# A hybrid decoder layer on one core: where the recurrent mixers stand beside the input projection, and how many tiles share a reciprocal root

## The chip, the cores and the metric

The kernel runs on one core of a Trainium2 chip. The metric is the device time of one execution in microseconds (us). The engines are TensorE (PE, with its weight loads shown as PEld), VectorE (DVE), ScalarE (ACT) and GpSimd (POOL); SyncE (SP) issues most DMAs. Each engine works through its own instructions in a fixed order and waits where an operand, a buffer or a DMA is not there yet. PE's granted clock is given as a share of full speed.

## The reference

One layer over 2048 tokens of width 1024, all in float32:

```python
h = _rms(x, norm_mix_g)
z = h @ w_in + b_in                       # 3600 columns
(a_q, a_k, a_v, a_f, b_qk, b_v, b_i, b_f, b_o, c_q, c_f, c_i, c_g) = _split_cols(z)
oa = _fox_attention(_rms(a_q), _rms(a_k), a_v, cumsum(log_sigmoid(a_f)))    # 8 heads of 64
qb, kb = split(silu(causal_conv4(b_qk)))
ob = _mlstm_chunkwise(qb, kb, b_v, b_i, b_f)                                # 4 heads of 64
oc = _hgrn2_chunkwise(silu(c_q), logf(c_f), c_i)                            # 4 heads of 64
y  = concat(_rms(oa)*g, sigmoid(b_o)*_rms(ob)*g, silu(c_g)*_rms(oc)*g)
x  = x + y @ w_out
x  = x + conv_glu(_rms(x, norm_ffn_g), w_up, ffn_conv_w, ffn_conv_b, w_down)
```

mLSTM (`ob`) and HGRN2 (`oc`) are recurrent: a block of tokens needs the state that the block before left. Both need only their own columns of z. A head of the attention needs the q, k and v of all 2048 tokens.

## The kernel before

**Projection.** z is made in two halves of 1024 tokens. A half is two token blocks of 512, whose x tiles (128 tokens each) are loaded, normed, transposed on PE and split into a high and a low part (`z_norm`, `norm_to_T`). `z_groups` then goes through 14 column groups in the order of the table `ORDER[hf]`. The weights of a group come in through the two buffers `wraw`, are cast on ACT and split on POOL (`load_split`); every product is three matmuls (`mm3`, high x high, high x low, low x high). Ten groups (`nat_group`) put tokens on the partitions and take 192 matmuls of up to 264 columns; b0, b1, c0 and c1 (`ct_group`) put columns there and take 96 matmuls of 512. A half is thus 2304 matmuls, all of them on one line, L166. bo, ci, cg, bv, b0, b1, c0 and c1 feed the recurrent mixers, k0, k1, q0, q1, v0 and v1 the attention; either set is 1152 matmuls a half. Results go to DRAM (`s_n`, `s_bqk`, `s_c`, `s_qh`, `s_kh`, `s_v` and so on) and are read back from there. A q or k tile is first normed per head of 64 (`qk_norm_T`): a reciprocal root on DVE in a chain of dependent small instructions (`rms_scale`, L109 to L120), one chain for each tile of 256 tokens.

**Mixers.** `mixers` runs four blocks of 512 tokens, each `phase_b` (mLSTM) with `phase_c` (HGRN2); a block starts when its eight groups are ready. Their tiles in PSUM are called b.

**Attention.** `attention` goes head by head in two passes, row maxima first and scores behind them; the first pass leads by 22 steps (`LEAD`). It begins when both halves are projected, since the pools of the projection are closed first. Then come w_out and the gated feed-forward part.

**What sets the order.** `merge(main, side, rate)` writes out `rate` steps of the mixers for each step of the projection; what is left of the mixers is written out with the attention, two of its steps for each of theirs. A scheduler in the build then fixes each engine's order by a simulated timeline of its own, among what the buffers allow. Before, half 0 is projected by itself, with the mixers' groups first; half 1 is projected with the mixers beside it, the attention's groups first:

```python
for _ in z:
    pass
merge(z_groups(k, 1, pz, wp, psw, (xb, xw)), mix, RZ)      # RZ = 2.5
...
for _ in mix:
    for _ in range(RA):                                    # RA = 2
        next(att, None)
```

The x tiles of half 0 and of half 1's first block go through buffers of the mixers' pool (v and p4, four in all), those of half 1's second block through wraw.

Of the kernel before, what the change touches and what calls it, by code (L numbers as in the profile page):

```python
# [9 lines left out]
F32 = mybir.dt.float32  # L10
F32R = mybir.dt.float32r
# [3 lines left out]
AF = mybir.ActivationFunctionType  # L15
ALU = mybir.AluOpType
# [23 lines left out]

RZ, RA = 2.5, 2

# [5 lines left out]
    "bo ci cg bv b0 b1 c0 c1 k0 k1 q0 q1 v0 v1",  # L48
    "k0 k1 q0 q1 v0 v1 ci cg bo bv b0 b1 c0 c1",
)  # L50
# [71 lines left out]

def norm_to_T(k, pool, psum, ptag, x, gb, hi, lo, tok, xn=None):

    nc = k.nc
    ss = k.t(pool, [P, 1], tag="nss")
    if xn is None:
        xn = k.t(pool, [P, D], tag="xn")
        junk, src = xn, x
    else:  # L130
        junk, src = lo[:, :, tok : tok + P], x.rearrange("p (a t) -> p a t", t=P)
    nc.scalar.activation(junk, src, AF.Square, accum_out=ss)
# [36 lines left out]
def z_norm(k, hf, b, pz, psum, xbufs):  # L169

    hi = k.t(pz, [P, DT, BLK], F32R, tag="hhi")
    lo = k.t(pz, [P, DT, BLK], F32R, tag="hlo")
    for tt in range(4):
        t0 = hf * HALF + b * BLK + tt * P
        xp, tag, bufs = xbufs[tt % len(xbufs)]
        x = k.t(xp, [P, D], tag=tag, bufs=bufs)
        k.nc.sync.dma_start(x, k.a["x"][0, t0 : t0 + P, :])
        if t0 == 0:
            k.nc.sync.dma_start(k.gmix, k.a["norm_mix_g"][0:1, :].broadcast_to([P, D]))
        norm_to_T(k, pz, psum, "t", x, k.gmix, hi, lo, tt * P, xn=x)  # L180
    return hi, lo


def z_groups(k, hf, pz, wp, psum, xbufs):
# [22 lines left out]
    def nat_group(off, kind, g):  # L207
# [6 lines left out]
        for b in range(2):  # L214
# [3 lines left out]
            for tp in range(2):  # L218
# [80 lines left out]

def qk_norm_T(k, pz, psum, z, kind, g, t0):  # L300
# [4 lines left out]
    z8 = z.rearrange("p tt (h d) -> p (tt h) d", d=HD)  # L305
    nc.scalar.activation(sq, z8, AF.Square)
    ss = k.t(pz, [P, 8], tag="ss")
    nc.vector.tensor_reduce(ss, sq, axis=AX.X, op=ALU.add)
    rstd = k.t(pz, [P, 8], tag="rstd")
    rms_scale(k, pz, rstd, ss, HD, 1.0, "h")  # L310
    nc.gpsimd.tensor_tensor(z8, z8, rstd.unsqueeze(2).broadcast_to([P, 8, HD]), op=ALU.mult)
    gcol = k.gq if kind == "q" else k.gk
    dhi, dlo = (k.s_qh, k.s_ql) if kind == "q" else (k.s_kh, k.s_kl)
    ps = k.t(psum, [P, 2, 2 * P], tag="t", bufs=2)
    for c in range(2):
        for tt in range(2):
            nc.tensor.transpose(
                ps[:, c, tt * P : (tt + 1) * P],
                z[:, tt, c * P : (c + 1) * P],
                k.ident,  # L320
            )
    lo = k.t(pz, [P, 2, 2 * P], F32R, tag="l", bufs=2)
    nc.scalar.activation(hi, ps, AF.Copy, scale=gcol)
    nc.vector.scalar_tensor_tensor(lo, ps, gcol, hi.bitcast(F32), op0=ALU.mult, op1=ALU.subtract)
    for dst, src in ((dhi, hi), (dlo, lo)):
        nc.sync.dma_start(
            dst[g * 256 : (g + 1) * 256, t0 : t0 + 2 * P].rearrange("(c p) t -> p c t", p=P), src.bitcast(F32)
        )

# [1002 lines left out]
def _trunk(ctx, tc, a, out):  # L1332
# [37 lines left out]
    with ExitStack() as ms:  # L1370
# [13 lines left out]
        with ExitStack() as zs:  # L1384
# [6 lines left out]
            next(z)  # L1391
            pz.tile([P, 8], F32, tag="padz", name="padz", bufs=1)
            state(k, mconst)
# [93 lines left out]
def consts(k, a, cp, mconst, pz, psum, cm):  # L1487
# [102 lines left out]
```

## Time and profile before

| | |
|---|---|
| median of 3 runs | 2981.64 us (2981.16 to 2985.46) |
| the profiled execution's own time | 2982.74 us |
| its span | 2981.0 us |
| PE busy, over the span | 2834.5 us (95%) |
| DVE, ACT, POOL busy | 2055.0 (69%), 1255.0 (42%), 1412.5 us (47%) |
| mean granted clock of PE | 0.975 |

The shares are averages over stages with different limits, so the stages have to be read one by one. Here the layer is cut at the times where one kind of work ends: half 0's mixers' groups to 220 us, half 0's attention's groups to 372, half 1's attention's groups to 585, half 1's mixers' groups to 820, attention with mixers beside it to 1143, attention alone to 1490, and the rest to the end.

### The profile page before, as it was taken

The page shows a single profiled execution, that of the slowest core. Times are in us where ns is not written, and L with a number is a line of the kernel's source. Part 1 is how long each engine was busy: PE and PEld are TensorE (multiplying, and loading weights), DVE is VectorE, ACT ScalarE, POOL GpSimd, SP SyncE. Part 2 cuts the span into 40 slices and gives each one's busy share as a digit, 9 for nine tenths or more (in the row PEclk, how much of TensorE's full clock was granted, in tenths as well). Part 3 has the DMA queues.
Part 4 walks back from the last instruction along what each step waited for, and adds up shares of the span by engine and source line. Part 5 has one row for each costly group of instructions (what it writes and reads, how often), then busy time and mean ns, then how long its engine had stood idle before and what let it go on. Part 6 is the DMA issues. An engine that isn't in the chain of part 4 may idle for free. (4 is left out here: it accounts for less than half of the span.)

```text
span 2981.0 us, 43125 instructions
## 1 busy us (share of the span) xinstructions
PE 2834.5 (95%) x15181; PEld 2350.0 (79%) x15181; DVE 2055.0 (69%) x3637; ACT 1255.0 (42%) x2138; POOL 1412.5 (47%) x1149
## 2 busy tenths in 40 slices
PE   7999999899978988899999999999999999999999
PEld 7889989899766665566688778888878888888887
DVE  6426688757379886777746567777697677777655
ACT  3232332312225456677623344444454344444443
POOL 2233434643245556756501176666476544444443
PEclk9999999999988889999999999999999999999999
DMA  5333434433261334433056634544677433333666
GB/s 170 115 113 123 148 106 128 144 93 94 93 149 49 77 66 97 100 71 66 18 182 212 198 129 163 161 157 155 222 263 260 155 105 105 100 102 124 226 206 214
DMA packets 332025, 406.88 MB, mean 136 GB/s; under 512 B 31010, under 2 KB 219504, under 8 KB 328640
## 3 DMA queue, kind: packets, MB, share of 16 engines
q1 hardware_dynamic: 296192, 335.37, 37.5%
q10 hardware_dynamic: 33264, 60.37, 5.4%
q0 software_dynamic: 2352, 8.39, 1.0%
q8 instruction: 119, 1.95, 0.3%
q14 instruction: 98, 0.80, 0.1%
HBM read 276.05 MB, written 127.98 MB: 136 GB/s over the span
## 5 line engine op out<-in xcount | busy, mean ns | idle before, releaser
L1027 POOL TENSOR_TENSOR w<-w,w 128x512 fp32r<-128x512 f32 x302 | 405.0, 1354 | 400.2 <-ACT w L1026 286.1
L1215 PE MATMUL ps<-w,w 128*128 128x512 f32 x1848 | 421.2, 390 | 4.4 <-ACT w L1206 1.9
L1215 PEld LDWEIGHTS ps<-w,w 128*128 128x128 f32 x1848 | 346.6, 188 | 78.2 <-POOL w L1208 2.6
L166 PE MATMUL w<-whi,hhi 128*128 128x256 f32 (+1 forms) x1280 | 369.4, 289 | 2.1 <-DVE pg L228 1.5
L166 PE MATMUL w<-wlo,hhi 128*128 128x256 f32 (+1 forms) x1280 | 367.7, 288 | 0.6 <-POOL wlo L157 0.6
L166 PE MATMUL w<-whi,hlo 128*128 128x256 f32 (+1 forms) x1280 | 367.0, 287 | 0.0
L783 POOL TENSOR_TENSOR pl<-pf,ph 128x512 fp32r<-128x512 f32 (+1 forms) x224 | 269.3, 1214 | 175.6 <-ACT ph L780 113.0
L1208 POOL TENSOR_TENSOR w<-w,w 128x512 fp32r<-128x512 f32 x154 | 215.4, 1405 | 204.4 <-ACT w L1206 172.3
L1026 ACT ACTIVATE w<-w 128x512 fp32r<-128x512 f32 x302 | 180.7, 627 | 261.0 <-POOL w L1027 82.5
L1207 DVE TENSOR_TENSOR w<-w,w 128x512 fp32r<-128x512 f32 x154 | 180.5, 1182 | 104.7 <-ACT w L1205 103.2
L166 PEld LDWEIGHTS w<-whi,hhi 128*128 128x128 f32 x1280 | 246.9, 193 | 3.7 <-issue 2.0
L166 PEld LDWEIGHTS w<-wlo,hhi 128*128 128x128 f32 x1280 | 246.7, 193 | 1.8 <-POOL wlo L157 1.0
L166 PEld LDWEIGHTS w<-whi,hlo 128*128 128x128 f32 x1280 | 246.4, 193 | 0.2
L745 DVE TENSOR_REDUCE mx<-m 128x1 f32<-128x512 f32 (+2 forms) x320 | 188.3, 604 | 63.6 <-PE m L740 36.2
L778 ACT ACTIVATE pf<-s 128x512 f32<-128x512 f32 (+1 forms) x320 | 168.4, 539 | 144.1 <-DVE pl L783 49.9
L157 POOL TENSOR_TENSOR wlo<-wraw,whi 128x1024 fp32r<-128x1024 f32 (+1 forms) x56 | 137.9, 2483 | 170.6 <-ACT whi L156 167.7
L1032 DVE TENSOR_TENSOR w<-w,w 128x512 f32<-128x512 f32 x176 | 151.2, 878 | 81.5 <-DMA w<-in_w_up_dram 69.4
L780 ACT ACTIVATE ph<-pf 128x512 fp32r<-128x512 f32 (+1 forms) x320 | 178.1, 575 | 45.8 <-PE pv L798 38.5
L1073 DVE SCALAR_TENSOR_TENSOR u<-ps,fcol,u 128x1023 f32<-128x1023 f32 x88 | 108.9, 1278 | 91.6 <-ACT u L1072 91.6
L771 PE MATMUL s<-QB,KB 70*128 70x512 f32 (+1 forms) x320 | 134.1, 419 | 30.7 <-ACT pf L778 30.3
L740 PE MATMUL m<-KB,QB 70*128 70x512 f32 (+2 forms) x320 | 135.3, 438 | 21.1 <-DVE mx L745 12.4
L1206 ACT ACTIVATE w<-w 128x512 fp32r<-128x512 f32 x154 | 96.7, 628 | 114.3 <-PE ps L1215 89.5
(349 smaller groups left out, 7102.1 us busy)
## 6 DMA issues: line engine op xcount, KB each, us to landing
w<-in_w_up_dram SPq DMA_DIRECT2D x182, 256.0 KB
w<-s_g SPq DMA_DIRECT2D x154, 256.0 KB
w<-in_w_down_dram SPq DMA_DIRECT2D x110, 256.0 KB
wraw<-in_w_in_dram SPq DMA_DIRECT2D x48, 512.0 KB
s_g<-u ACTq DMA_DIRECT2D x88, 256.0 KB
w<-s_w SPq DMA_DIRECT2D x88, 256.0 KB
s_g<-w ACTq DMA_DIRECT2D x66, 256.0 KB
w<-s_h SPq DMA_DIRECT2D x48, 256.0 KB
```

Source lines behind the costliest of these rows:

```text
L157: nc.gpsimd.tensor_tensor(lo[:, q : q + n, :], raw, h.bitcast(F32), op=ALU.subtract)
L166: nc.tensor.matmul(out, lsl(lhs[a], i), rsl(rhs[b], i), start=(i == 0 and j == 0), stop=(i == n - 1 and j == 2))
L745: nc.vector.tensor_reduce(mx[:, i, kb : kb + 1], ps[:, 0:n], axis=AX.X, op=ALU.max)
L778: nc.scalar.activation(pf[:, c0:], ps[:, c0:], AF.Exp)
L780: nc.scalar.activation(ph[:, c0:], pf[:, c0:], AF.Copy)
L783: eng.tensor_tensor(pl[:, c0:], pf[:, c0:], ph[:, c0:].bitcast(F32), op=ALU.subtract)
L1026: nc.scalar.activation(h, t, AF.Copy)
L1027: nc.gpsimd.tensor_tensor(lo, t, h.bitcast(F32), op=ALU.subtract)
L1032: nc.vector.tensor_tensor(t, x, y, op=op)
L1207: nc.vector.tensor_tensor(gl, gr, gh.bitcast(F32), op=ALU.subtract)
L1208: nc.gpsimd.tensor_tensor(wl, wr, wh.bitcast(F32), op=ALU.subtract)
L1215: nc.tensor.matmul(tiles[tile], g[x][:, tile * P : (tile + 1) * P], w[y], start=j == 0 and c == 0, stop=j == nj - 1 and c == 2,)
```

## The change

1. Half 1 projects the mixers' groups first, like half 0, and its attention's groups in another order.
2. The mixers are merged into the projection from half 0 on, at 2.2 steps for each step of the projection, and at 4.7 steps once c1 of half 1's first block has been projected (`k.ready["c1"] >= 3`).
3. Reciprocal roots are made for several tiles in one chain: two q or k tiles (16 columns in place of 8), and the x tiles that there are buffers for (4 in half 0's second block, 2 in half 1). All tiles of a chain are held until it is done.
4. Both blocks of half 1 take their x tiles through the two wraw buffers.

```diff
-RZ, RA = 2.5, 2
+RZ0, RZ1, RA = 2.2, (2.2, 4.7), 2
 ORDER = (
     "bo ci cg bv b0 b1 c0 c1 k0 k1 q0 q1 v0 v1",
-    "k0 k1 q0 q1 v0 v1 ci cg bo bv b0 b1 c0 c1",
+    "bo ci cg bv b0 b1 c0 c1 v1 v0 k0 q0 k1 q1",
 )
+def norms_to_T(k, pool, psum, ptag, xs, gb, hi, lo, tok):
+    nc = k.nc
+    n = len(xs)
+    ss = k.t(pool, [P, 4], tag="nss")[:, 0:n]
+    for i, x in enumerate(xs):
+        t = tok + i * P
+        nc.scalar.activation(
+            lo[:, :, t : t + P], x.rearrange("p (a t) -> p a t", t=P), AF.Square, accum_out=ss[:, i : i + 1]
+        )
+    rstd = k.t(pool, [P, 4], tag="nrs")[:, 0:n]
+    rms_scale(k, pool, rstd, ss, D, 1.0, f"n{n}")
+    for i, x in enumerate(xs):
+        nc.vector.scalar_tensor_tensor(x, x, rstd[:, i : i + 1], gb, op0=ALU.mult, op1=ALU.mult)
+        to_T(k, psum, ptag, x, hi, lo, tok + i * P)
...
+    n = 1 if hf == b == 0 else sum(bufs for _, _, bufs in xbufs)
+    for t in range(0, 4, n):
...
-                    qk_norm_T(k, pz, psum, z, kind, g, t0)
+                    if tp == 0:
+                        zs, ss = [], k.t(pz, [P, 16], tag="ss")
+                    zs.append((z, qk_squares(k, pz, z, ss[:, 8 * tp : 8 * tp + 8]), t0))
+                    if tp == 1:
+                        qk_norm_T(k, pz, psum, zs, ss, kind, g)
...
-        due += rate
+        due += rate()
...
-            for _ in z:
-                pass
-            merge(z_groups(k, 1, pz, wp, psw, (xb, xw)), mix, RZ)
+            merge(z, mix, lambda: RZ0)
+            merge(z_groups(k, 1, pz, wp, psw, (xw, xw)), mix, lambda: RZ1[k.ready["c1"] >= 3])
```

What the edits make of the order shows at three places. The first is PE in half 0's k1, at the 1248th matmul of the projection, where before only matmuls of the projection (w) stand:

```order
L166 MATMUL w_2066<-wlo_1972,hhi_106 128x256
L166 MATMUL w_2066<-whi_1971,hlo_107 128x256
L166 MATMUL w_2148<-whi_1971,hhi_482 128x256
L166 MATMUL w_2148<-wlo_1972,hhi_482 128x256
L166 MATMUL w_2148<-whi_1971,hlo_483 128x256
```

At the same place the changed kernel has mixers' matmuls (b) between two tiles of the projection (whose line is now L185):

```order
L185 MATMUL w_2111<-wlo_2013,hhi_106 128x256
L185 MATMUL w_2111<-whi_2012,hlo_107 128x256
L530 MATMUL b_2203<-b_qk_1876 128x128
L530 MATMUL b_2204<-b_qk_1876 128x128
L678 MATMUL b_2213<-q_94,c_2093 128x128 x4
L185 MATMUL w_2224<-whi_2012,hhi_482 128x256
L185 MATMUL w_2224<-wlo_2013,hhi_482 128x256
```

Of the mixers' 728 matmuls before (182 for a block), half 0's attention's groups had none beside them, half 1's first 1152 projection matmuls had 198, its last 1152 had 184, and 346 came behind the projection. Now the four numbers are 192, 186, 253 and 97.

The second place is PE at the boundary of the halves, behind half 0's last projection matmul (w_3861). Before, the transposes of the first x tile (t, out of v) stand there, then mixers' matmuls, and the first matmul of half 1 (w_4089) comes before the second x tile's transposes (out of p; some of the mixers' rows between are left out):

```order
L166 MATMUL w_3861<-whi_3469,hlo_483 128x264
L265 MATMUL w_3900<-ident,pg_3764 36x128 x3
L140 MATMUL t_3941<-ident,v_3923 128x128 x4
L140 MATMUL t_3948<-ident,v_3923 128x128 x4
L452 MATMUL b_4205<-ident,rows_4200 128x12 x4
L615 MATMUL b_4428<-q_94,c_4415 128x256 x2
L166 MATMUL w_4089<-whi_4076,hhi_3921 128x256
L166 MATMUL w_4089<-wlo_4077,hhi_3921 128x256
L140 MATMUL t_3973<-ident,p_462_3955 128x128 x4
```

Now two x tiles (out of wraw) stand ahead of that matmul here, and the other two ahead of these, with mixers' matmuls between (59 of them from half 0's last projection matmul to half 1's first, w_4673):

```order
L678 MATMUL b_4738<-q_94,c_4318 96x128 x4
L159 MATMUL t_4614<-ident,wraw_4590 128x128 x4
L159 MATMUL t_4621<-ident,wraw_4590 128x128 x4
L536 MATMUL b_4796<-bstate,b_qk_4072 128x130 x2
L678 MATMUL b_4805<-q_94,c_4318 64x128 x4
L548 MATMUL b_4875<-v_4180,e_4647 128x65 x4
L159 MATMUL t_4629<-ident,wraw_4592 128x128 x4
L159 MATMUL t_4636<-ident,wraw_4592 128x128 x4
L553 MATMUL b_4938<-v_4180,p_603_4522 128x130
L185 MATMUL w_4673<-whi_4660,hhi_4535 128x256
```

What moved is the x tiles' way: the first projection matmul of half 1 now stands behind all of the first block's transposes.

The third place is SP where the projection ends and the first head's q and k (QB, KB) are read back. Before, no store of q or k stands near:

```order
L588 DMA ld_9844<-s_c 128x512
L715 DMA V_9011<-s_v 128x16x130
L871 DMA woraw_13450<-in_w_out_dram 128x1024
L697 DMA ld_10828<-s_n 128x2x256
L1408 DMA ga<-in_out_g_dram 128x512
L715 DMA QB_9009<-s_qh 64x2048
L715 DMA KB_9010<-s_kh 64x2048
```

Now the last stores of q (s_qh, s_ql) stand right ahead of that read:

```order
L750 DMA V_9777<-s_v 128x16x130
L361 DMA s_qh<-h_9581 128x2x256
L361 DMA s_ql<-l_9660 128x2x256
L361 DMA s_qh<-h_9635 128x2x256
L361 DMA s_ql<-l_9671 128x2x256
L1442 DMA ga<-in_out_g_dram 128x512
L750 DMA QB_9775<-s_qh 64x2048
L750 DMA KB_9776<-s_kh 64x2048
```

The read of the first head's q thus moved from long after q's last store to directly behind it.

## Rows read from the trace of the kernel before

**Rows 1.** Busy time by engine in the stages named above: the stretch, the sum of its length, then for each engine busy us with the number of instructions, PE's granted clock, the share of the DMA engines and GB/s.

```profile
core 0: us, PE busy (x) PEld busy (x) DVE busy (x) ACT busy (x) POOL busy (x), PEclk, DMA share, GB/s
0.00:220.00 220.00, 199.86 (x1229) 180.88 (x1230) 103.15 (x230) 66.84 (x94) 52.09 (x32) 0.98 0.42 135
220.00:372.00 152.00, 150.49 (x1252) 149.39 (x1251) 98.48 (x312) 50.65 (x79) 62.16 (x78) 1.00 0.41 132
372.00:585.00 213.00, 199.61 (x1619) 191.13 (x1618) 179.59 (x488) 71.44 (x124) 98.20 (x117) 1.00 0.41 127
585.00:820.00 235.00, 227.47 (x1505) 205.59 (x1503) 128.23 (x253) 61.13 (x91) 83.79 (x63) 0.99 0.30 94
820.00:1143.00 323.00, 274.69 (x1461) 203.04 (x1460) 268.57 (x539) 145.42 (x291) 173.31 (x155) 0.87 0.35 82
1143.00:1490.00 347.00, 315.82 (x1580) 210.56 (x1579) 250.94 (x475) 240.23 (x463) 218.30 (x173) 0.96 0.34 72
1490.00:2981.00 1491.00, 1466.53 (x6544) 1209.39 (x6543) 1026.03 (x1343) 619.32 (x997) 724.67 (x534) 0.99 0.52 172
```

**Rows 2.** The same view, of the projection's matmuls (L166) alone: a stretch with groups of 192 matmuls (half 0's attention's groups), and one inside b0 to c1 (matmuls of 512 columns).

```profile
core 0: us, PE busy (x) PEld busy (x), PEclk, DMA share, GB/s
220.00:372.00 152.00, 143.03 (x1153) 139.46 (x1151) 1.00 0.41 132
150.00:200.00 50.00, 50.00 (x222) 41.42 (x221) 1.00 0.34 106
```

**Rows 3.** The same view, of the mixers' PSUM tile b alone, in the three stages with mixers; 1345 PE records in all, 336 for each of the four blocks.

```profile
core 0: us, PE busy (x) PEld busy (x) DVE busy (x) ACT busy (x), PEclk, DMA share, GB/s
372.00:585.00 213.00, 49.94 (x342) 40.66 (x336) 32.47 (x72) 6.79 (x21) 1.00 0.41 127
585.00:820.00 235.00, 48.65 (x340) 41.58 (x336) 34.36 (x76) 6.50 (x20) 0.99 0.30 94
820.00:1143.00 323.00, 105.50 (x644) 91.55 (x637) 61.82 (x137) 12.34 (x39) 0.87 0.35 82
```

**Rows 4.** Lines of the timeline (start, duration, both in us): the attention's first matmul, the last step of its second head, its last transposes; and, from the groups by line, the mixers' stores (first and last start behind the comma) and the row maxima of the attention's first pass, which head by head runs ahead of the scores.

```profile
837.27 0.51 PE L740 MATMUL m<-KB,QB 70*128 70x256 f32 x1
...
1119.68 2.75 POOL L832 TENSOR_TENSOR asq<-asq,ga 128x1024 f32<-128x1024 f32 x1 [0.64 <-DVE asq L831]
...
1489.86 0.46 PE L806 MATMUL m<-ident,oT 65*128 65x65 f32 x4 [0.68 <-ACT oT L803]
...
L572 POOL DMA_DIRECT2D s_y<-p x4: 792/795/804, 593.7 to 1143.3; - x4
...
L745 DVE TENSOR_REDUCE mx<-m 128x1 f32<-128x512 f32 (+2 forms) x320 | 188.3, 604 | 63.6 <-PE m L740 36.2
```

**Rows 5.** Timeline at the boundary of half 1's two blocks, where x tiles already go through wraw: the load of two x tiles, the first weight load behind them, a pair of later weight loads with the cast of the second one's weights, and one x tile's four transposes.

```profile
418.56 4.99 SPq L177 DMA_DIRECT2D wraw<-in_x_dram  x2
...
437.50 0.37 SPq L154 DMA_DIRECT2D wraw<-in_w_in_dram  x1
...
451.80 4.57 SPq L154 DMA_DIRECT2D wraw<-in_w_in_dram  x2
456.48 1.06 ACT L156 ACTIVATE whi<-wraw 128x1024 fp32r<-128x1024 f32 x1 [2.99 <-DMA wraw<-in_w_in_dram]
...
372.56 0.66 PE L140 MATMUL t<-ident,p 128*128 128x128 f32 x4
```

**Rows 6.** Timeline of one q tile (its bias added, its last store issued), the landing time of a store by its median, and the reads of the first head's q in the attention.

```profile
318.45 0.69 DVE L242 TENSOR_TENSOR z<-w,bias 128x512 f32<-128x512 f32 x1 [0.59 <-PE w L166]
...
332.34 0.37 SPq L326 DMA_DIRECT2D s_ql<-l  x1
...
s_y<-b_qk POOLq DMA_DIRECT2D x4, 512.0 KB, 3.5
...
825.30 0.53 SPq L715 DMA_DIRECT2D QB<-s_qh  x1
```

**Rows 7.** DVE's groups by line from the start to 1160 us: the first and the last of the 41 groups that belong to the mixers, which sum to 361.3 us. Behind the bar: busy us, mean ns of one.

```profile
L428 DVE SCALAR_TENSOR_TENSOR c<-ld,col,c 128x512 f32<-128x512 f32 x48 | 53.5, 1115 | 21.2 <-ACT c L426 20.5
...
L421 DVE MEMSET ld<- 128x3 f32 x4 | 0.2, 61 | 0.1
```

**Rows 8.** Four steps of the q and k tiles' root chains by line (16 chains a half; L118 and L120 stand three times in a chain): the first four rows are half 0's (220 to 372 us, no mixers), the other four half 1's (372 to 585 us, mixers beside them).

```profile
L111 DVE TENSOR_SCALAR rstd<-hm 128x8 int32<-128x8 int32 x16 | 11.2, 698 | 0.5
L118 DVE TENSOR_TENSOR hu<-rstd 128x8 f32<-128x8 f32 x48 | 8.0, 166 | 1.5
L120 DVE SCALAR_TENSOR_TENSOR rstd<-hu,rstd 128x8 f32<-128x8 f32 x48 | 8.0, 166 | 1.5
L109 DVE TENSOR_SCALAR hm<-ss 128x8 f32<-128x8 f32 x16 | 3.5, 218 | 0.6
...
L111 DVE TENSOR_SCALAR rstd<-hm 128x8 int32<-128x8 int32 x16 | 4.6, 285 | 1.4 <-POOL z L311 1.0 <-DVE rstd L111 0.3
L118 DVE TENSOR_TENSOR hu<-rstd 128x8 f32<-128x8 f32 x48 | 13.0, 277 | 0.8
L120 DVE SCALAR_TENSOR_TENSOR rstd<-hu,rstd 128x8 f32<-128x8 f32 x48 | 9.5, 201 | 0.9
L109 DVE TENSOR_SCALAR hm<-ss 128x8 f32<-128x8 f32 x16 | 11.0, 686 | 0.1
```

More of the change, by code (lines that the diff above doesn't have):

```diff
@@ L120, in rms_scale, with norm_to_T @@
         nc.vector.scalar_tensor_tensor(out, u, 1.5, out, op0=ALU.add, op1=ALU.mult)
-def norm_to_T(k, pool, psum, ptag, x, gb, hi, lo, tok, xn=None):
+def norm_to_T(k, pool, psum, ptag, x, gb, hi, lo, tok):
     nc = k.nc
     ss = k.t(pool, [P, 1], tag="nss")
[L127 to L132, printed above, removed]
+    xn = k.t(pool, [P, D], tag="xn")
+    nc.scalar.activation(xn, x, AF.Square, accum_out=ss)
     rstd = k.t(pool, [P, 1], tag="nrs")
@@ L135, in norm_to_T, with to_T @@
     nc.vector.scalar_tensor_tensor(xn, x, rstd, gb, op0=ALU.mult, op1=ALU.mult)
+    to_T(k, psum, ptag, xn, hi, lo, tok)
+def norms_to_T(k, pool, psum, ptag, xs, gb, hi, lo, tok):
[12 more added lines that the diff above has]
+        to_T(k, psum, ptag, x, hi, lo, tok + i * P)
+def to_T(k, psum, ptag, xn, hi, lo, tok):
+    nc = k.nc
     for q in range(2):
@@ L172, in z_norm @@
     lo = k.t(pz, [P, DT, BLK], F32R, tag="hlo")
[L173 to L180, printed above, removed]
+    n = 1 if hf == b == 0 else sum(bufs for _, _, bufs in xbufs)
+    for t in range(0, 4, n):
+        xs = []
+        for tt in range(t, t + n):
+            t0 = hf * HALF + b * BLK + tt * P
+            xp, tag, bufs = xbufs[tt % len(xbufs)]
+            x = k.t(xp, [P, D], tag=tag, bufs=bufs)
+            k.nc.sync.dma_start(x, k.a["x"][0, t0 : t0 + P, :])
+            if t0 == 0:
+                k.nc.sync.dma_start(k.gmix, k.a["norm_mix_g"][0:1, :].broadcast_to([P, D]))
+            xs.append(x)
+        norms_to_T(k, pz, psum, "t", xs, k.gmix, hi, lo, t * P)
     return hi, lo
@@ L297, in z_groups, with qk_squares @@
                 break
-def qk_norm_T(k, pz, psum, z, kind, g, t0):
+def qk_squares(k, pz, z, ss):
     nc = k.nc
@@ L304, in qk_norm_T @@
     sq = hi.bitcast(F32).rearrange("p c (a d) -> p (c a) d", d=HD)
-    z8 = z.rearrange("p tt (h d) -> p (tt h) d", d=HD)
-    nc.scalar.activation(sq, z8, AF.Square)
-    ss = k.t(pz, [P, 8], tag="ss")
+    nc.scalar.activation(sq, z.rearrange("p tt (h d) -> p (tt h) d", d=HD), AF.Square)
     nc.vector.tensor_reduce(ss, sq, axis=AX.X, op=ALU.add)
-    rstd = k.t(pz, [P, 8], tag="rstd")
+    return hi
+def qk_norm_T(k, pz, psum, zs, ss, kind, g):
+    nc = k.nc
+    rstd = k.t(pz, [P, 16], tag="rstd")
@@ L310, in qk_norm_T @@
     rms_scale(k, pz, rstd, ss, HD, 1.0, "h")
-    nc.gpsimd.tensor_tensor(z8, z8, rstd.unsqueeze(2).broadcast_to([P, 8, HD]), op=ALU.mult)
     gcol = k.gq if kind == "q" else k.gk
     dhi, dlo = (k.s_qh, k.s_ql) if kind == "q" else (k.s_kh, k.s_kl)
[L314 to L320, printed above, removed]
-            )
@@ L322, in qk_norm_T @@
[L322 to L328, printed above, removed]
+    for n, (z, hi, t0) in enumerate(zs):
+        z8 = z.rearrange("p tt (h d) -> p (tt h) d", d=HD)
+        r8 = rstd[:, 8 * n : 8 * n + 8].unsqueeze(2).broadcast_to([P, 8, HD])
+        nc.gpsimd.tensor_tensor(z8, z8, r8, op=ALU.mult)
+        ps = k.t(psum, [P, 2, 2 * P], tag="t", bufs=2)
+        for c in range(2):
+            for tt in range(2):
+                nc.tensor.transpose(
+                    ps[:, c, tt * P : (tt + 1) * P],
+                    z[:, tt, c * P : (c + 1) * P],
+                    k.ident,
+                )
+        lo = k.t(pz, [P, 2, 2 * P], F32R, tag="l", bufs=2)
+        nc.scalar.activation(hi, ps, AF.Copy, scale=gcol)
+        nc.vector.scalar_tensor_tensor(lo, ps, gcol, hi.bitcast(F32), op0=ALU.mult, op1=ALU.subtract)
+        for dst, src in ((dhi, hi), (dlo, lo)):
+            nc.sync.dma_start(
+                dst[g * 256 : (g + 1) * 256, t0 : t0 + 2 * P].rearrange("(c p) t -> p c t", p=P), src.bitcast(F32)
+            )
@@ L1391, in _trunk @@
             next(z)
-            pz.tile([P, 8], F32, tag="padz", name="padz", bufs=1)
+            pz.tile([P, 24], F32, tag="padz", name="padz", bufs=1)
             state(k, mconst)
```

4 lines of the change are left out of this document (2 added, 2 removed).

## The prediction, as put on record before the changed kernel ran

> **What bounds the kernel now.** I read the stages first [rows 1], since the share over the span hides them. From 1490 us PE is busy 1467 of 1491 us; nothing there is changed, so I take that stretch over as it is, with the 1.7 us by which the execution's own time (2982.7) exceeds its span. That execution is 1.1 us above the median of the three runs. What can move lies before 1490. Of the four quarters of the projection (1152 matmuls each) half 0's attention's groups, which have nothing beside them, fill PE: 150.5 of 152 us. The two quarters with mixers are nearly full too (199.6 of 213, 227.5 of 235). The loose stage is 820 to 1143, attention with mixers: PE busy 274.7 of 323 us at a granted clock of 0.87, DVE 268.6 of 323. So the question is what a block of mixers costs beside the projection and what beside the attention.
>
> *Beside the projection.* 1152 matmuls of 256 columns take 152 us, 0.132 each; in b0 to c1, PE is full with 222 in 50 us, 0.225 each [rows 2]. The mixers' groups are 768 of the one kind and 384 of the other: 101 + 87 = 188 us. Half 1's took 235 with 340 of 336 b records, 1.01 blocks [rows 3]: 47 us a block. PE's own busy time on b there says the same, 48.65 us. It also accounts for the other quarter with mixers: 152 + 1.02 × 47 + 16 x transposes of 0.66 [rows 5] = 211, and it took 213 [rows 1]. In the projection a block of mixers costs PE's time and little else.
>
> *Beside the attention.* From the end of the second head (1119.7) to the last transposes (1489.9) six heads take 370, 61.7 each [rows 4]. Two heads by themselves would be 123, and 13 more for the 22 row maxima of 0.60 by which the first pass leads: 137. They took 1119.7 − 837.3 = 282. The excess, 146, belongs to 644/336 = 1.92 blocks [rows 3]: 76 us a block. The mixers' stores of this stage run to 1143 [rows 4], so it is theirs to the end. A block moved from there into the projection thus gains 76 − 47 = 29 us.
>
> **The change part by part.** The order gives the blocks: 192, 186, 253 and 97 of 182 matmuls, that is 1.05, 1.02, 1.39 and 0.53.
>
> First quarter, half 0's mixers' groups: no mixers, 220 us as now [rows 1].
>
> Second quarter, half 0's attention's groups: 152 + 1.05 × 47 = 201.
>
> Third quarter, half 1's mixers' groups: 188 + 1.02 × 47 = 236, and 10.6 for the 16 transposes of x, which used to stand in the other quarter. New is the wait at its start: x tiles three and four can only be loaded into wraw when tiles one and two have been transposed, and the first weights only behind those. The chain stands in the trace, at the block boundary where x tiles go through wraw already [rows 5]: load issued 418.56, weights issued 437.50, so 18.9; from there to the start of the cast 4.7, and 1.1 for it: 25 us. The 59 mixers' matmuls that stand there, 0.32 block, fill 15. I take 10, with bounds 0 (they and the transposes cover it, and tiles one and two are loaded long before) and 25. Sum 257.
>
> Fourth quarter, half 1's attention's groups with 1.39 blocks: by PE 152 + 1.39 × 47 = 217. DVE now comes close: these groups took 98.5 us of it in half 0 [rows 1], a block of mixers a quarter of 361.3 [rows 7], so 98.5 + 1.39 × 90 = 224; of the 16 root chains eight vanish, of whose four steps that I read (30.7 us) [rows 8] half goes, 15: 209 us. Nowhere with mixers did DVE pass 84% (179.6 of 213) [rows 1]; at that share 209 take 248. That was reached where PE set the pace, so it is a bound and no price. Between 217 and 248 I take the middle, 232.
>
> The projection then ends at 220 + 201 + 257 + 232 = 910, in place of 820.
>
> The way into the attention: now 820 to 837 [rows 1, 4]. In the changed order the last q stores stand directly ahead of the read of q. A q tile took from its bias (318.45) to its last store (332.34) 13.9, a store lands in 3.5, and from the issue of the read (825.30) to the first matmul (837.27) are 12.0 [rows 4, 6]: 29, with the rest 30, and 17 is the lower bound. In these 30 the mixers run with DVE to themselves: 30/90 = 0.33 of the last 0.53 block. What is left, 0.2 × 76 = 15, falls on the attention.
>
> The attention by itself: 137 + 370 = 507. The end of it: 910 + 30 + 507 + 15 = 1462, 28 earlier than 1490, and 1462 + 1491 + 1.7 = 2955; against the median 2954.
>
> The batched chains are put at nothing elsewhere: the second quarter's 15 us of DVE lie beside a full PE (DVE 98.5 of 152 before [rows 1], about 98.5 − 15 + 95 = 178 of 201 now). Without that cover they would give 15 at most. A pair of q tiles is held until its chain is done; with three z buffers PE could wait for one, but a chain is twelve short steps and the next tile has 48 matmuls, 6.3 us, to run. I put that at nothing as well; by the 13.9 us above [rows 6] it could cost a few us a pair, eight pairs in a half, which is inside the bounds of the fourth quarter.
>
> **The rivals.**
> *Larger gain.* PE paces all four quarters, the mixers cover the boundary wait and the way into the attention stays at 17: 220 + 201 + 247 + 217 = 885, then 17, with 0.19 block done in it and 0.34 × 76 = 26 left: 885 + 17 + 507 + 26 = 1435, so 2928. For it speaks that 47 us fits both quarters with mixers; against it the order at the boundary and the q stores.
>
> *No change.* Beside attention's groups a block costs 60, not 47: (213 − 152)/1.02 [rows 1, 3], if the x tiles' norms there cost nothing of their own. Then 220 + 215 + 259 + 235 = 929, with DVE's bound in the last quarter 942: the end is at 1481 to 1494, the time 2974 to 2987.
>
> *Slower.* The mixers' own chain of dependent steps paces the fourth quarter. Beside attention's groups they went through 198 of 182 matmuls, 1.09 blocks by the order, in 213 us, 195 a block; 1.39 of these are 271, 39 more than I took: 2994. It decides from 266 us on, 191 a block (28 of gain and 6 for a measurable loss above 232). Against it: beside the attention 1.92 blocks took 323 us [rows 1, 3], 168 a block, which would be 234. For it: that quarter of the old kernel had DVE at 84% already, and the new one asks 4.7 steps of the mixers for each of the projection.
>
> *Slower by contention.* In half 1 the chains' steps cost more than in half 0: L109's mean went from 218 to 686 ns and L118's from 166 to 277, while L111's fell from 698 to 285; the four steps from 30.7 to 38.1, by a factor of 1.24 [rows 8]. If all of DVE's work in the fourth quarter stretched like that, 209 would be 259 and at 84% 307, 75 above my 232: 3030. The trace has too little of it, since PE hardly waited (199.6 of 213). [...]
>
> **How the numbers follow.** Forecast 0.46, its own range 2929 to 2973; larger gain 0.22; no change 0.11; slower by the chain 0.17; by contention 0.04. 2912 to 2998 leaves out the far part of the larger gain (perhaps a third of it, 0.07), what of the slower chain lies higher, and contention, under 0.2 in all. About 0.2% (6 us) is what a measurement of this kernel can tell from no change. Faster by more: forecast 0.45, larger gain 0.22, a fifth of no change: 0.69. Within: 0.10, most of no change and the near edge of slower. Slower: 0.21.
>
> **What would show it.** The trace of the changed kernel, cut at each 1152 projection matmuls, should have stages of 220, 201, 257 and 232 us. In the second and third PE is full but for some 10 us at the halves' boundary; in the fourth the idle time before PE's projection matmuls, if any, should be put down to DVE. The first matmul of the attention should stand near 940, the mixers' last store within some 30 us of it; the first two heads should take 137 + 15 and the later ones 62 each. From the end of the attention (near 1462) 1491 must be left. A fourth quarter above 266, heads that stay at 70 or more without mixers, or a boundary of more than 25 us with PE idle would prove me wrong.

## The result: 0.9% faster, with errors of both signs inside the sum

The changed kernel takes 2957.77 us (median of four runs, 2950.22 to 2958.81) against 2981.4; the ratio is 0.9912, with an interval of 0.9894 to 0.9931. The forecast was 2954. Its four quarters, the way into the attention and the attention itself can be laid beside the trace, cut at every 1152 projection matmuls as the prediction asked. The columns are those of [rows 1]; the stages are the four quarters of the projection, the way from its last matmul to the attention's first, the attention, and the rest.

```profile
core 0: us, PE busy (x) PEld busy (x) DVE busy (x) ACT busy (x) POOL busy (x), PEclk, DMA share, GB/s
0.00:215.40 215.40, 197.94 (x1231) 179.13 (x1231) 96.59 (x207) 66.98 (x95) 52.14 (x32) 0.99 0.42 133
215.40:412.90 197.50, 190.92 (x1571) 184.71 (x1571) 149.92 (x344) 59.94 (x103) 94.85 (x114) 1.00 0.37 116
412.90:680.70 267.80, 247.02 (x1575) 220.70 (x1573) 153.10 (x313) 79.75 (x123) 93.70 (x75) 0.96 0.36 111
680.70:893.90 213.20, 207.15 (x1686) 199.73 (x1684) 163.22 (x371) 64.23 (x111) 111.66 (x124) 0.99 0.32 103
893.90:921.20 27.30, 17.95 (x101) 13.91 (x100) 19.93 (x48) 4.02 (x9) 9.70 (x11) 0.81 0.72 192
921.20:1460.60 539.40, 499.37 (x2490) 339.52 (x2491) 401.03 (x774) 361.44 (x702) 323.53 (x262) 0.94 0.37 78
1460.60:2948.40 1487.80, 1465.05 (x6541) 1207.89 (x6539) 1025.48 (x1341) 619.91 (x997) 727.13 (x534) 0.99 0.53 172
```

| stage | forecast | this profile | a second profile of the same kernel |
|---|---|---|---|
| first quarter | 220 | 215.4 | 215.6 |
| second | 201 | 197.5 | 196.7 |
| third | 257 | 267.8 | 262.3 |
| fourth | 232 | 213.2 | 213.9 |
| way into the attention | 30 | 27.3 | 27.3 |
| attention with the mixers' rest | 522 | 539.4 | 542.1 |
| end of the attention | 1462 | 1460.6 | 1457.9 |
| rest | 1491 | 1487.8 | 1493.1 |

The rest holds only unchanged code, and between the profiles of this study it lies anywhere from 1488 to 1501 us. That scatter is as large as the smaller effects below, so beside the times I compare where the attention ends.

### The profile page after: what moved, and what is told of

Same layout as the page of the kernel before. It is cut to its first block, busy times and chain, and to the rows that moved or that the text cites. A ratio compares the mean times of both kernels' runs of the same rounds, so it can differ in the third digit from the quotient of the medians.

```text
span 2948.4 us, 42870 instructions
## 1 busy us (share of the span) xinstructions
PE 2825.4 (96%) x15181; PEld 2345.6 (80%) x15181; DVE 2009.3 (68%) x3397; ACT 1256.3 (43%) x2138; POOL 1412.7 (48%) x1149
## 3 DMA queue, kind: packets, MB, share of 16 engines
q1 hardware_dynamic: 296192, 335.37, 38.2%
## 5 line engine op out<-in xcount | busy, mean ns | idle before, releaser
L185 PE MATMUL w<-whi,hhi 128*128 128x256 f32 (+1 forms) x1280 | 373.0, 292 | 1.7 <-ACT whi L175 1.4
L185 PE MATMUL w<-wlo,hhi 128*128 128x256 f32 (+1 forms) x1280 | 368.7, 288 | 0.7 <-POOL wlo L176 0.7
L185 PE MATMUL w<-whi,hlo 128*128 128x256 f32 (+1 forms) x1280 | 368.4, 288 | 0.0
L185 PEld LDWEIGHTS w<-whi,hhi 128*128 128x128 f32 x1280 | 247.2, 193 | 3.9 <-ACT whi L175 1.6
L185 PEld LDWEIGHTS w<-wlo,hhi 128*128 128x128 f32 x1280 | 247.4, 193 | 2.0 <-POOL wlo L176 1.1
L185 PEld LDWEIGHTS w<-whi,hlo 128*128 128x128 f32 x1280 | 246.8, 193 | 0.6
```

What stands on the lines that cost most here:

```text
L185: nc.tensor.matmul(out, lsl(lhs[a], i), rsl(rhs[b], i), start=(i == 0 and j == 0), stop=(i == n - 1 and j == 2))
```

## The experiments

Each undoes or moves one thing, starting from the changed kernel unless it says otherwise. The kernel before, run on the same chips, stood between 2983 and 2987, so ratios are what to compare; the changed kernel run again gave 0.9909 (0.9892 to 0.9925).

> The changed kernel as it is, beside the next three on one chip: 0.991 of the kernel before, about 2957.

### One chain for each tile: part of the gain goes

```diff
-    n = 1 if hf == b == 0 else sum(bufs for _, _, bufs in xbufs)
+    n = 1
...
-                    if tp == 0:
-                        zs, ss = [], k.t(pz, [P, 16], tag="ss")
-                    zs.append((z, qk_squares(k, pz, z, ss[:, 8 * tp : 8 * tp + 8]), t0))
-                    if tp == 1:
-                        qk_norm_T(k, pz, psum, zs, ss, kind, g)
+                    ss = k.t(pz, [P, 8], tag="ss")
+                    qk_norm_T(k, pz, psum, [(z, qk_squares(k, pz, z, ss), t0)], ss, kind, g)
...
```

> The changed kernel with one reciprocal root chain for each tile, as before (batching undone, order and rates kept). My theory: the gain comes from mixers' blocks moved out of the attention's stage, the batched chains give nothing, so 2958 within 6 us. The rival (batched chains free VectorE, and that is the gain): 2972 to 2982, and half 1's last quarter of the projection, 213 us in the changed kernel, becomes 225 or more.

2971.49 us, ratio 0.9956 (0.9941 to 0.997): half of the gain is gone, against my theory. The 225 us that the rival wanted in the last quarter did not come either. The quarters were 222.0, 193.5, 263.7 and 220.4, the attention ended at 1474.7. The same view of its first and fourth quarter and of the attention:

```profile
0.00:222.00 222.00, 200.67 (x1231) 179.35 (x1231) 103.19 (x231) 67.23 (x95) 52.13 (x32) 0.98 0.41 129
...
679.20:899.60 220.40, 208.38 (x1681) 199.10 (x1679) 182.55 (x467) 62.82 (x109) 107.37 (x124) 0.98 0.33 103
...
923.90:1474.70 550.80, 494.19 (x2505) 334.69 (x2505) 401.50 (x781) 364.51 (x703) 328.38 (x266) 0.95 0.36 76
```

The first quarter is 6.6 us longer, and the only thing that differs in it is the x tiles of half 0's second block, four chains in place of one. The fourth is 7 us longer with 19 us more of DVE (182.55 against 163.22). The attention is 9 to 11 us longer and the way into it 3 shorter, 6 to 8 together; that is more than these two edits explain.

### The batched chains by themselves: no change

The kernel before with edit 3 alone.

> The kernel before with the batched chains alone (old order of the groups, mixers from half 1 on, x tiles of half 1's first block in the mixers' pool). My theory: within 6 us of 2981. The rival by VectorE (it loses 46 us of busy time): about 2960.

2983.16 us, ratio 0.9998 (0.9985 to 1.001). The first quarter falls here too, to 215.5, but half 1's first quarter loses it again: cut at 1152 projection matmuls, it goes from 217.4 to 223.6 us. The longest stretch of PE without a projection matmul in it, at the boundary between half 1's two blocks, was 16.3 us before and is now 24.7; both as windows, first the kernel before:

```profile
401.30:417.60 16.30, 11.06 (x88) 9.27 (x87) 15.09 (x41) 4.98 (x7) 7.60 (x11) 1.00 0.22 76
```

and the batched one:

```profile
400.40:425.10 24.70, 19.61 (x134) 16.87 (x133) 20.32 (x55) 6.98 (x12) 12.38 (x16) 0.86 0.22 75
```

Two x tiles share a chain there and there are two buffers, so none is free before both are done. Whether that is what lengthens the stretch is not shown. PE is idle for 5 us of it in both kernels and the rest is filled with other matmuls, at a granted clock of 0.86 and not 1.00; and the kernel with the old order (below), with the same pairs in the same two buffers, has a stretch of 16.9 us there.

### Which of the tiles it is: half 1's x tiles, and the pairs

```diff
-    n = 1 if hf == b == 0 else sum(bufs for _, _, bufs in xbufs)
+    n = 1 if hf or b == 0 else sum(bufs for _, _, bufs in xbufs)
```

> The changed kernel with a root chain of its own for each x tile of half 1 (q and k pairs still batched). At the boundary of the halves PE has no projection matmul for 39 us. If the two-tile chain on two buffers makes that wait (no tile can leave before both are done), it falls to 30 or less and the time by 8 or more us, to 2949. If VectorE paces the boundary (it is busy 38 of 46 us there), the wait stays at 36 or more and the time within 5 us of the changed kernel; then the 13 us that single chains everywhere cost lie with the q and k pairs and with half 0's x tiles (its first quarter took 222, not 215).

2951.54 us, 0.9888 (0.9873 to 0.9903), against 2956.01 of the changed kernel beside it; the intervals overlap. The 38 us without projection matmuls at the boundary stayed (37.8). So it is not the chain's width that makes this wait.

> The changed kernel with one chain for each q and k tile again; the x tiles stay batched. If the pairs are what the batching is worth (15 us less of VectorE's time in half 1's last quarter, where its work comes close to PE's), about 2966 and a last quarter of 219 to 221 us, not 213. If the x tiles' batching is worth it, 2957 and 213.

2961.53 us, 0.9916 (0.9902 to 0.993), no measurable difference from the changed kernel, but the fourth quarter moved as the expectation has it, to 219.9:

```profile
671.20:891.10 219.90, 207.74 (x1680) 199.07 (x1679) 181.50 (x467) 62.55 (x109) 107.33 (x124) 0.98 0.33 104
```

6 us are lost there, and about 4 gained in the second quarter (193.2, and 193.5 with single chains everywhere, where the changed kernel has 197.5 and 196.7): that is what the pairs cost there, which the prediction had put at nothing. In sum the attention ended at 1462, 1 to 4 us later. Both effects are real in the stages and nearly cancel. By the ratios all single chains together cost 14 us; these parts account for 8 to 11 (6.6 in the first quarter, 1 to 4 for the pairs, nothing or a gain for half 1's x tiles). What makes the other few us of the attention in that run stays open.

### Mixers from half 1 on only: slower than before

```diff
-            merge(z, mix, lambda: RZ0)
+            for _ in z:
+                pass
-            merge(z_groups(k, 1, pz, wp, psw, (xw, xw)), mix, lambda: RZ1[k.ready["c1"] >= 3])
+            merge(z_groups(k, 1, pz, wp, psw, (xw, xw)), mix, lambda: 2.5)
```

> The changed kernel with the mixers merged from half 1 on only (rate 2.5), new order of half 1 kept. By the build's order 1.23, 1.34 and 1.43 blocks stand in half 1's first quarter pair, last pair and behind the projection. My theory (29 us for each block moved): quarters 217, 152, 278 and 213, then 27 us, 1.1 blocks at 76 on the attention, in all about 2972. The rival that the new order of the groups alone brings the gain: 2958.

2997.61 us, 1.0043 (1.0028 to 1.0058): slower than the kernel before, over 20 us above my expectation, and no gain from the order alone. The projection ended at 853, sooner than I had put it. The miss is behind it:

```profile
853.00:894.00 41.00, 28.05 (x140) 24.32 (x138) 30.02 (x84) 8.07 (x17) 15.81 (x19) 0.65 0.63 157
894.00:1500.80 606.80, 541.61 (x2733) 372.20 (x2734) 456.99 (x888) 375.62 (x726) 358.10 (x293) 0.92 0.34 74
```

The way into the attention is 41 us and not 27, at a granted clock of 0.65, with DVE busy for 30 of them, and the attention takes 607. Together 648, where the changed kernel has 567 and 569 with 0.84 block of mixers less behind the projection. Tile b in the same two windows (columns as in [rows 3]):

```profile
853.00:894.00 41.00, 26.58 (x130) 22.68 (x128) 12.44 (x27) 2.76 (x9) 0.65 0.63 157
894.00:1500.80 606.80, 58.07 (x338) 49.16 (x334) 32.99 (x74) 6.52 (x20) 0.92 0.34 74
```

### Half the rate in half 0: the price of a block left behind

```diff
-RZ0, RZ1, RA = 2.2, (2.2, 4.7), 2
+RZ0, RZ1, RA = 1.1, (2.2, 4.7), 2
```

> The changed kernel with the mixers merged into half 0 at half the rate (1.1 in place of 2.2). By the build's order 0.59, 1.28, 1.26 and 0.87 blocks stand in the second to fourth quarter and behind the projection, in place of 1.06, 1.01, 1.34 and 0.59, so 0.28 block goes back to the attention. By my theory a moved block is worth 29 us: 2964 (8 us above the changed kernel), the projection ending 13 us earlier and the rest taking 21 longer. By the kernel with no mixers in half 0, whose 0.85 block behind the projection cost 79 us there (93 a block) and gave 38 back, a block is worth 48: 2970.

2973.89 us, 0.9956 (0.9943 to 0.997), which is 2968 where the kernel before takes 2981.4: nearer to the second price than to mine. The second to fourth quarter have 0.56, 1.35 and 1.26 blocks. Tile b on the way and behind it (columns as in [rows 3]):

```profile
886.20:924.10 37.90, 27.12 (x123) 22.50 (x120) 11.07 (x28) 2.84 (x8) 0.58 0.63 163
924.10:1481.00 556.90, 27.39 (x157) 23.30 (x156) 14.99 (x33) 3.26 (x11) 0.95 0.35 75
```

Behind the projection stand 280 records, 0.83 block, and 595 us; the changed kernel has 184, 0.55 (below), and 568; the kernel with late mixers 466, 1.39, and 648. That is 27 us for 0.28 block and 53 for 0.56: some 95 a block between single profiles of the new order, where the prediction had 76 from the old one. Part of it is paid on the way (38 and 41 us, not 27): the last store of q is issued 15.7 us behind the projection's last matmul in the changed kernel, 22.7 here and 27.6 with late mixers, and the attention's first matmul follows it after 12 to 15. The rest is paid in the attention. By the ratios this run loses 13 us against the changed kernel for its 0.28 block and the one with late mixers 40 for 0.84, so moving a block out of the attention's stage is worth about 48 us, as the second price has it.

### Old order of half 1, mixers from half 0 on: slower

> The changed kernel with half 1's groups in the old order, mixers from half 0 on. By the build's order 1.06, 0.96, 0.12 and 1.87 blocks stand in the second, third and fourth quarter and behind the projection: the mixers lack half 1's groups until the end. My theory: nothing is moved out of the attention's stage and the wait at the halves' boundary is still paid, quarters about 217, 198, 240 and 194, then 17 and 142 us of mixers on the attention: about 2990. The rival that an early start of the mixers brings the gain by itself: 2965 or less.

2991.82 us, 1.0028 (1.0017 to 1.0039), as forecast. The quarters were 215, 196, 230 and 195, and 1.83 blocks remained for the attention, which took 640. An early start by itself moves nothing out of that stage: the mixers then wait for half 1's groups. With the run with late mixers this shows that, beside edits 3 and 4, neither edit 1 nor edit 2 is a gain by itself, and that the two together are. Both runs keep the x tiles of half 1 in the wraw buffers (edit 4) and so pay the wait at the halves' boundary; no run takes edit 4 back alone.

### X tiles of half 1 written out 25 us earlier: faster than both

```diff
+        if n == 26 and early is not None:
+            next(early)
...
+            z1 = z_groups(k, 1, pz, wp, psw, (xw, xw))
-            z = z_groups(k, 0, pz, wp, psw, (xb, xb))
+            z = z_groups(k, 0, pz, wp, psw, (xb, xb), z1)
...
-            merge(z_groups(k, 1, pz, wp, psw, (xw, xw)), mix, lambda: RZ1[k.ready["c1"] >= 3])
+            merge(z1, mix, lambda: RZ1[k.ready["c1"] >= 3])
```

> The changed kernel with the loads, norms and transposes of half 1's first x tiles written out before the last two groups' second block of half 0, some 25 us earlier; nothing else is changed, and the blocks of mixers in each quarter are the same by the build's order. If the chain of loads through the two wraw buffers is what PE waits for at the boundary, the 39 us without projection matmuls fall to about 15 to 20 and the time to 2935 to 2942. The rival (the mixers' matmuls that now fill this time have to be done anyway, at VectorE's pace): within 6 us of the changed kernel.

2946.73 us, 0.9872 (0.9856 to 0.9887). The stretch without projection matmuls fell from 39 to 18 us, but the third quarter only from 262 or 268 to 256.7, and the attention ended at 1451.3, 7 to 9 sooner. Both expectations were half right. The wait was the chain's, but the mixers filled most of it: PE was idle for 13 us of the 39 (14 in the second profile) and is idle for 6.5 of the 18. What the early tiles give back is about that difference. The stretch in the changed kernel, and then here (columns as in [rows 1]):

```profile
412.90:451.80 38.90, 25.83 (x152) 21.69 (x149) 34.74 (x74) 13.00 (x21) 19.36 (x27) 0.82 0.30 93
...
413.60:431.90 18.30, 11.75 (x65) 10.10 (x63) 18.23 (x31) 7.00 (x11) 10.24 (x16) 0.81 0.50 137
```

With the x tiles of half 1 in chains of their own on top of that:

> The kernel with the early x tiles (18 us without projection matmuls at the boundary, in place of 39) with a root chain of its own for each x tile of half 1. If the second pair's way through two buffers makes the rest of that wait, it falls to 12 or less and the time to about 2942; if not, 2947 as without it.

2949.86 us, 0.9878 (0.9863 to 0.9894). The stretch fell to 12.2, nearly as far as the expectation asked, and the time did not follow: PE's idle part of it fell only from 6.5 to 4.8 us.

### The v tiles last: the shorter way gains nothing

```diff
-    "bo ci cg bv b0 b1 c0 c1 v1 v0 k0 q0 k1 q1",
+    "bo ci cg bv b0 b1 c0 c1 v1 k0 q0 k1 q1 v0",
```

> The changed kernel with half 1's attention's groups in the order v1 k0 q0 k1 q1 v0: the last stores are those of v, not of q. The way from the last projection matmul to the attention's first is 27 us in the changed kernel, 17 before. If q's stores make the difference it falls to about 18 and the time by 5 to 9 us, to 2949 to 2953 (some of the mixers done in those us come back on the attention). The rival (the way is set by the mixers' work and the change of pools): 25 or more, no change.

2969.01 us, 0.9947 (0.9931 to 0.9962), 13 us slower than the changed kernel beside it (2956.01). The last quarter, the way and the attention:

```profile
677.20:895.30 218.10, 209.81 (x1694) 201.64 (x1692) 166.51 (x386) 65.66 (x112) 109.22 (x122) 0.98 0.34 105
895.30:911.10 15.80, 9.18 (x54) 7.41 (x52) 7.40 (x19) 2.15 (x7) 3.98 (x6) 0.87 0.90 224
911.10:1470.60 559.50, 501.96 (x2527) 340.39 (x2528) 413.83 (x788) 363.09 (x703) 326.80 (x268) 0.94 0.37 76
```

The way fell to 15.8 us, below what I had asked of it, so q's stores are what sets it: the last of them is now issued 2 us ahead of the projection's last matmul and not 16 behind it. But the attention grew by 17 to 20. In the changed kernel the mixers have 92 records of b on the way and 92 to 94 beside the attention, here 52 and 132, so some 40 (0.12 block) came back on it. At 95 us a block that is 11 of the 17 to 20; what the others are, and why the last quarter is 4 to 5 us longer as well, no run here shows. Behind the projection this kernel has the same 0.55 block as the changed one and takes 575 us, not 567 to 569. So nothing here says that a block is cheaper beside the attention when the q tiles do not come last.

### The mixers' rest more thinly among the attention

The kernel with the early x tiles and `RA` 4 in place of 2.

> The kernel with the early x tiles and the mixers' rest merged into the attention at four of its steps for each of the mixers', not two. The 0.54 block left over then stands beside more of the attention. If a block's price there (76 us or more) comes from the mixers' chain holding up the first heads, it falls and the time goes to 2935 to 2942. If it is work that has to be done somewhere in this stage (VectorE's 90 us a block at PE's lower granted clock), the first head is faster, the next slower, and the time the same, 2947 within 4.

2942.81 us, 0.9856 (0.9843 to 0.987), the fastest of the study and clearly below the changed kernel's 0.9909. The attention ended at 1445.4, 6 us sooner than without it; the time itself does not differ measurably from that kernel's 0.9872.

```profile
908.50:1445.40 536.90, 494.70 (x2488) 335.27 (x2488) 400.80 (x770) 362.40 (x702) 324.72 (x262) 0.96 0.37 78
```

The attention takes 536.9 us, where it took 540.9; two profiles of the changed kernel differ by 2.7. So how the rest is merged is at most a small part of its price.

## Why the prediction was right, and where it was not

**The direction and the mechanism hold.** Mixers moved out of the attention's stage into the projection gain time, and beside the projection they cost little more than PE's own time on them (48.95 us for 1.03 blocks, 66.02 for 1.40: 47 each). The second quarter has 348 records of b, 1.03 blocks, in 197.5 us. The attention's groups with batched chains and no mixers take 145.7 (late mixers, below), so a block costs (197.5 − 145.7)/1.03 = 50 us there and (213.2 − 145.7)/1.40 = 48 in the fourth quarter. The 47 that came from the old kernel's fourth quarter was right within 3 us. Tile b in the same stages (columns as in [rows 3]):

```profile
215.40:412.90 197.50, 48.95 (x348) 40.71 (x343) 32.92 (x74) 6.75 (x21) 1.00 0.37 116
...
680.70:893.90 213.20, 66.02 (x470) 55.79 (x464) 45.42 (x99) 8.38 (x26) 0.99 0.32 103
...
893.90:921.20 27.30, 16.82 (x92) 12.99 (x90) 10.30 (x22) 1.50 (x5) 0.81 0.72 192
921.20:1000.00 78.80, 17.75 (x92) 16.17 (x92) 7.02 (x18) 2.09 (x8) 0.74 0.50 116
```

The 152 us to which the prediction added the 47 was read too long. The kernel before ends half 0's projection at 367.7, 147.5 us into that quarter (first line below); up to 372 PE does transposes of half 1's first x tile and mixers' matmuls:

```profile
367.42 0.28 PE L166 MATMUL w<-whi,hlo 128*128 128x264 f32 x1
...
367.87 1.04 PE L140 MATMUL t<-ident,v 128*128 128x128 f32 x8
...
372.05 0.47 PE L166 MATMUL w<-whi,hhi 128*128 128x256 f32 x1
```

So the second quarter's 201 came near 197.5 with a pure part 6 us too long and a block 3 us too cheap.

**First quarter, 5 us too long.** I carried it over as it was and put the batched x tiles of half 0's second block at nothing. That quarter was not full of PE in [rows 1] (199.9 of 220), and the trace of single chains against batched ones shows 222.0 against 215.4. The cover that I named was in the second quarter; the first had none.

**Third quarter, 5 to 11 us too short.** The step of the boundary had the right chain and too small a price. In the changed kernel, on SP, the x tiles that follow the first two, and then the weights:

```profile
418.60 0.97 SPq L200 DMA_DIRECT2D wraw<-in_x_dram  x1
...
421.46 0.33 SPq L200 DMA_DIRECT2D wraw<-in_x_dram  x1
...
446.59 8.10 SPq L173 DMA_DIRECT2D wraw<-in_w_in_dram  x3
```

On PE and ACT, the transposes of the first and the third of the four tiles, and the casts of the weights:

```profile
412.96 1.04 PE L159 MATMUL t<-ident,wraw 128*128 128x128 f32 x8
...
445.42 1.10 PE L159 MATMUL t<-ident,wraw 128*128 128x128 f32 x8
...
455.47 1.06 ACT L175 ACTIVATE whi<-wraw 128x1024 fp32r<-128x1024 f32 x1 [0.25 <-DMA wraw<-in_w_in_dram]
457.89 1.06 ACT L175 ACTIVATE whi<-wraw 128x1024 fp32r<-128x1024 f32 x1 [1.36 <-DMA wraw<-in_w_in_dram]
```

From the load's issue (418.60) to the weights' issue are 28 us, where [rows 5] had 18.9. The first projection matmul stands at 451.8, and steady projection begins at 459, 46 after the last matmul of half 0. The mixers stand in the chain's way, on DVE above all. The pair's root chain has twelve steps with 2.3 us of work; other instructions, most of them the mixers', stand between its first and its last and stretch it over 10.9 us:

```profile
431.98 0.63 DVE L109 TENSOR_SCALAR n2m<-nss 128x2 f32<-128x2 f32 x1
...
442.68 0.16 DVE L120 SCALAR_TENSOR_TENSOR nrs<-n2u,nrs 128x2 f32<-128x2 f32 x1
```

The whole stretch (columns as in [rows 1]):

```profile
412.90:459.00 46.10, 31.00 (x191) 26.36 (x188) 38.19 (x82) 16.65 (x27) 24.14 (x29) 0.85 0.35 107
```

DVE is busy 38.2 of 46.1 us, and PE idle for 15, not 10, at a granted clock of 0.85. That the mixers fill a wait and lengthen it at the same time was not in the sum.

**Fourth quarter, 19 us too long.** The failed step is the one that took the middle between PE's 217 and VectorE's 248. DVE had 163 us there, not 209, and PE 207 of 213: it was PE's alone. The 98.5 us that I took for the attention's groups were those of a stretch in which half 1's first x tiles were normed as well; the kernel with late mixers does these groups in half 0, with batched chains and only two x tiles normed among them, in 72 us of DVE (214.9 to 360.6):

```profile
214.90:360.60 145.70, 145.70 (x1222) 145.64 (x1222) 72.22 (x182) 42.32 (x66) 53.68 (x76) 1.00 0.39 128
```

That leaves 91 for 1.40 blocks, 65 each, in place of 90. A quarter of the mixers' DVE time goes with a quarter of their matmuls only on the mean over all stages. The lower bound of my range for this step, 217, was the better value, and the rival of the mixers' own pace (271) far off.

**The attention, 17 to 20 us too short, with errors of both signs in it.** What I took for the attention by itself was too long. The six heads behind the second take 349 us (1111.6 to 1460.6), where I read 370 from [rows 4]: five of 60.4 each, and a last one of 47. The first head's two windows, the second head, the third to seventh, and the last (columns as in [rows 1]):

```profile
921.20:970.00 48.80, 44.38 (x204) 33.36 (x204) 40.62 (x94) 17.24 (x36) 19.03 (x20) 0.71 0.67 144
970.00:1052.50 82.50, 70.52 (x321) 47.23 (x321) 57.47 (x99) 55.01 (x101) 59.05 (x41) 0.85 0.42 104
1052.50:1111.60 59.10, 57.45 (x297) 38.91 (x296) 41.40 (x81) 43.56 (x86) 36.09 (x30) 0.96 0.40 83
1111.60:1413.70 302.10, 284.59 (x1481) 192.29 (x1480) 230.94 (x427) 218.12 (x425) 181.97 (x150) 1.00 0.34 67
1413.70:1460.60 46.90, 42.43 (x193) 27.73 (x192) 30.60 (x77) 27.52 (x54) 27.39 (x23) 0.91 0.11 28
```

In the kernel before, the last steps of the third to the seventh head (that of the second is at 1119.68 [rows 4]) are these:

```profile
1194.73 2.39 POOL L832 TENSOR_TENSOR asq<-asq,ga 128x1024 f32<-128x1024 f32 x1 [1.16 <-DVE asq L831]
1260.58 2.39 POOL L832 TENSOR_TENSOR asq<-asq,ga 128x1024 f32<-128x1024 f32 x1 [1.58 <-DVE asq L831]
1323.94 2.37 POOL L832 TENSOR_TENSOR asq<-asq,ga 128x1024 f32<-128x1024 f32 x1
1382.81 2.39 POOL L832 TENSOR_TENSOR asq<-asq,ga 128x1024 f32<-128x1024 f32 x1 [2.28 <-DVE asq L831]
1443.73 2.39 POOL L832 TENSOR_TENSOR asq<-asq,ga 128x1024 f32<-128x1024 f32 x1 [2.82 <-DVE asq L831]
```

The third to fifth head take 75, 66 and 63 us, though the mixers' last store is at 1143, and only then come 59 and 61. The kernels with the old order and with the batched chains alone, which have nearly as many mixers left (1.83 and 1.91 blocks), have 72 and 66, and 73 and 70, for the third and fourth; the changed kernel and the one at half rate have 60 to 61 from the third head to the seventh, the one with late mixers 60 to 63. So the mean of 61.7 that I took for pure seems to hold 21 us that go with the mixers, and the price of 76 left them out. With heads of 60.4 the first two would be 134 with the lead; their excess is then 282 − 134 = 148, with the 21 it is 169, and a block costs 88. That these 21 us are an after-effect of the mixers is argued from this comparison; no run isolates it.

What I added for the mixers' rest, 15, is far more: the first two heads take 190 us, where I had 152. Nearly all of it lies in the first, 131 us to its end, where 60.4 and the lead would be 74; the second (59.1) is already at the pure pace. The mixers' last store is at 972, 51 us behind the attention's first matmul, not 30. PE is granted 0.71 of its clock up to 970 (busy 44.4 of 48.8 us) and 0.85 to 1052 (70.5 of 82.5). How much of the excess is the clock and how much DVE (40.6 of 48.8 us) I can't separate; the runs with a longer rest have lower clocks on the way too (0.58, 0.65).

**The sum was right partly by luck.** The price of a block beside the attention was too low and the fourth quarter too long: a moved block is worth some 48 us by the runs at half rate and with late mixers, not 29. In the profile the first two heads were 38 us longer than forecast and the third quarter 11; the fourth quarter was 19 shorter, the six later heads 21, the first two quarters 8 and the way 3. These errors all but cancel, so that the end of the attention came within 5 us of 1462.

**The rivals.** The larger gain had the fourth quarter nearly right (217) and was too short at the boundary (247), on the way (17) and for the leftover. Neither slower one came. The one without a change wanted 60 us a block beside the attention's groups, and the two quarters gave 50 and 48; with single chains everywhere the fourth takes 220.4, or 53 a block over the 147.5 without mixers, so that rival was nearer before the pairs than with them. What the rival by contention assumed was there in single steps and not in the sum: DVE had 163 us in the fourth quarter, not 259. The step L111 of the 16-column chains in the second quarter, then L118 and L111 in the fourth, and last L111 in half 0 of the kernel with late mixers (214.9 to 360.6), where no mixers stand beside it:

```profile
L111 DVE TENSOR_SCALAR rstd<-hm 128x16 int32<-128x16 int32 x8 | 8.0, 1000 | 0.0
...
L118 DVE TENSOR_TENSOR hu<-rstd 128x16 f32<-128x16 f32 x21 | 3.6, 173 | 0.4
L111 DVE TENSOR_SCALAR rstd<-hm 128x16 int32<-128x16 int32 x7 | 1.2, 173 | 0.0
...
L111 DVE TENSOR_SCALAR rstd<-hm 128x16 int32<-128x16 int32 x8 | 10.2, 1276 | 0.0
```

The same step takes 1000 ns and 173 in two stages with mixers beside it, and 1276 without any, so mixers are not needed to stretch it. What does, no run here isolates. At their shortest mean of a stage in the two kernels, L118 of the q and k chains took 173 ns with 16 columns (fourth quarter, above) and 166 with 8 [rows 8], L120 173 (second quarter) and 166; by these steps a wide chain costs little more than a narrow one does, and it replaces two.

## What to carry to other kernels

When the price of a piece of work is an excess over a pure part, take the pure part from a stretch that this work no longer touches: with heads of 60.4 us, not 61.7, a block of mixers beside the attention comes to 88 us and not 76. A run that moves a little of the work gives what moving it is worth directly (13 us for 0.28 block). When a stretch's busy time is carried to another place, first subtract what else stood in it, and cut the stretch where its last instruction ends (147.5 us, not 152). A wait that is filled with useful work gave back about its idle part when it was shortened: from 39 us to 18 PE's idle part fell by 7 and the attention ended 7 to 9 us sooner; from 18 to 12 it fell by 2 and nothing was gained.

## What the runs showed of the hardware that was not expected

TensorE's granted clock fell to 0.58 and 0.65 in stretches of about 40 us in which it was busy for 29 and 28 us, and to 0.71 where it was busy 44.4 of 48.8, while it stayed at 1.00 in the second quarter of the changed kernel (busy 190.9 of 197.5) and at 0.99 in the fourth (207.2 of 213.2). One step of the q and k tiles' root chains on DVE, L111 with 16 columns, took from 173 to 1276 ns on the mean of a stage, and the longest with no mixers beside it. The stretch from the attention's end on, in which no instruction's work was changed, took from 1487.8 to 1501.1 us over the profiles of this study.
